# Input sums of the feed-forward's block products moved into the norming of token tiles and through DRAM, with the last down weights in other buffers

## The chip, the cores and the metric

One core of one Trainium2 chip runs the whole program. The metric is the device time of one execution in microseconds (us). The kernel before takes 3409.91 us, the median of three runs (3407.55 to 3410.49).

## What is computed

The reference is one step of a two-layer trunk on 256 context tokens and 1024 latent tokens of width 1024. Layer 0 mixes with a gated MLP and grouped-query attention, layer 1 with neighbourhood attention; after each mixer comes a SwiGLU feed-forward. Every sub-layer is normed before and after, and shifted, scaled and gated by six vectors that come from a conditioning vector (`mod_w`, `mod_b`). All arrays are float32. What the change touches is the output of a mixer and the feed-forward behind it:

```python
def sublayer_in(x, g, shift, scale):
    return rms_norm(x, g) * (1 + scale) + shift

def sublayer_out(x, y, g, gate):
    return x + gate * rms_norm(y, g)

def swiglu(h, w_in, w_out):
    g, u = jnp.split(h @ w_in, 2, axis=-1)
    return (jax.nn.silu(g) * u) @ w_out
```

with `w_in` of 1024 x 5632 and `w_out` of 2816 x 1024.

## The kernel before, in words

**Numbers.** A float32 operand is kept as two float32r parts, `hi` (a cast, on ACT) and `lo` (the rest, a subtraction on DVE or POOL); `split` (lines 168 to 176) makes both. A product is three matmuls: hi·hi, hi·lo, lo·hi. The normed, modulated activations of all 1280 tokens lie in `hh` and `hl`, eight blocks of 128 features by ten tiles of 128 tokens. Tiles 0 and 1 are the context, 2 to 9 the latents.

**Output projection and norms.** `out_proj` (line 1107) takes the token tiles in the order 4, 5, 6, 7, 8, 9, 2, 3, 0, 1 through a software pipeline: `load` (the attention output from DRAM and its split; layer 1 has it in `hh`/`hl` already), `product` (PE), `norms` (ACT's sums of squares, POOL's power at line 214, DVE's lines 414, 415 and 358) and `cols`. `cols` calls `prenorm_pair`: eight PE transposes (line 385), eight ACT passes (line 388) and the split into `hh`/`hl`; for an odd tile the features 0 to 511 first have the even tile of the pair subtracted (line 394). `cols` of tiles 0 and 1 is not done there but inside the feed-forward, as `before[0]` and `before[1]`. The subtraction of a split goes to POOL in layer 0 and to DVE in layer 1. Here the framework orders each engine's instructions itself, by program order and by when it thinks that they are ready.

**Feed-forward, up.** `ffn` (line 1168) makes gate and up projection of 128 + 128 columns of the 22 blocks `m` by seven block products (Strassen's scheme in Winograd's form) in place of eight: inputs are two halves of features by even and odd tiles, weights two halves of features by gate and up. Products 1, 5, 2 and 3 (`FREE`) read `hh`/`hl` as they are. Products 6, 7 and 4 (`BOUND`) need sums of input blocks, which `sums` (line 1174) forms once for each feed-forward: eight calls (four feature blocks by two token sets, set 0 = tiles 4 to 9, 384 columns for each product, set 1 = tiles 0 to 3, 256 columns). A call is seven DVE instructions (lines 1183 to 1191 and two split subtractions), three POOL (1187, 1188, 176) and three ACT casts. `weights` splits the weight block for a product, `weight_sums` (1206) forms the weight sums. PSUM has three banks of tag B, two double banks of tag A and one bank C. For the first two `m` all `FREE` products of set 0, then of set 1, then all `BOUND` ones run; from `m` = 2 on it is product by product. All of it stands in one hand-written list of (position, function) pairs, which are sorted by position (`at`, lines 1290 to 1341) and issued in that order on each engine (`weave`). `behind(("SP","DVE","PE"))` keeps the list's instructions on these three queues behind the last ones of `out_proj`; ACT and POOL have no such edge.

**Fillers.** `extra` runs steps of `mod_half_steps` (line 300): the next modulation vectors, by DVE multiply-adds (lines 320, 322), two small PE matmuls (327) and copies. In the main loop it is called once at even products and for two steps at odd ones. Layer 0's feed-forward carries six vectors (12 halves), layer 1's one.

**Feed-forward, down.** `gu_d` holds the 22 result blocks in DRAM. `down_load` (line 1348) loads and splits the weights and results of a pair of blocks. Pairs 0 to 7 are added up pair by pair over ten token tiles, and the last three pairs (`LAST = 3`) in one group, so that each tile is done and normed as it comes. The weights of a pair lie in the eight `wt` buffers, those of the last pair in `s5`, and the loads of pairs 9 and 10 come behind the loop and behind both `gate_load`s. Buffers: `wt` 8 x 4096 bytes for each partition, `raw` 3 x 4096, `s5` 17 x 5120, `t2` 5 x 2048.

**DMA.** All transfers are issued on SP's queue, in order: one that waits holds up those behind it.

Of the kernel before, what the change touches and what calls it, by code (L numbers as in the profile page):

```python
# [11 lines left out]
F32 = mybir.dt.float32  # L12
# [6 lines left out]
P = 128  # L19
# [30 lines left out]
def trunk_kernel(ctx: ExitStack, tc: tile.TileContext, A: dict, O: dict):  # L50
# [257 lines left out]
    def mod_half_steps(l, part):  # L308

        w, what = part // 3, part % 3  # L310
        for j in range(2):
            total = [t2([P, 512]) for _ in range(2)]
            for k in range(0, KT, 2):
                r = s5([P, 2, 512])
                SP.dma_start(r, A["mod_w"][l, k * P : k * P + 256, part * D + 512 * j : part * D + 512 * j + 512].rearrange("(b p) n -> p b n", b=2))
                yield
                for b in range(2):
                    for c in range(2):
                        if k + b == 0:
                            DVE.tensor_scalar(total[c], r[:, b], cond[:, k + b, c : c + 1], None, op0=ALU.mult)  # L320
                        else:
                            DVE.scalar_tensor_tensor(total[c], r[:, b], cond[:, k + b, c : c + 1], total[c], op0=ALU.mult, op1=ALU.add)  # L322
                    yield
            res, acc = t2([32, 512]), bank2()
            SP.dma_start(res, A["mod_b"][l, part, 32 * j : 32 * j + 32])
            for c in range(2):
                PE.matmul(acc[0:32, 0:512], pick[:, c, :], total[c], start=c == 0, stop=c == 1)
            yield
            DVE.tensor_tensor(res, acc[0:32, 0:512], res, op=ALU.add)
            yield  # L330
            if what == 2:
# [12 lines left out]
            yield  # L344
# [33 lines left out]
    def prenorm_pair(t, xh, l, w, lo):  # L378

        trs = []  # L380
        for _ in range(2):
            tr = bank((P, 4, P))
            trs += [tr[:, k, :] for k in range(4)]
# [5 lines left out]
        if t % 2 == 0:  # L389
            split(hh[:, :, rows(t)], hl[:, :, rows(t)], xh, lo, DVE)  # L390
        else:
            split(hh[:, 4:8, rows(t)], hl[:, 4:8, rows(t)], xh[:, 4:8], lo, DVE)
            for x in (hh, hl):
                DVE.tensor_tensor(xh[:, 0:4], xh[:, 0:4], f32(x[:, 0:4, rows(t - 1)]), op=ALU.subtract)
            split(hh[:, 0:4, rows(t)], hl[:, 0:4, rows(t)], xh[:, 0:4], lo, DVE)
# [712 lines left out]
    def out_proj(l, w, xsrc, dst, early=None):  # L1108

        w0, w1 = w[:4], w[4:]  # L1110
        gate = {}

# [32 lines left out]
        def cols(t):  # L1145
            prenorm_pair(t, st.pop(("xh", t)), l, 1, DVE if early else POOL)

        late = OUT_ORDER[-2:]
# [19 lines left out]
    def ffn(l, ubase, xsrc, dst, extra, before, after=()):  # L1168


        more, size = [], [(c.stop - c.start) * P for c in SETS]
        place = [slice(c.start * P, c.stop * P) for c in SETS]

        def sums(s, k):

            if not more:
                more.extend([[s5([P, 2, 640], F32R) for _ in range(2)] for _ in range(2)] for _ in range(3))
            q, n, c = SETS[s], size[s], place[s]
            tmp = s5([P, 3, n])
            x, d, z = (tmp[:, i].rearrange("p (q f) -> p q f", f=P) for i in range(3))  # L1180
            parts = [[more[i][a][k // 2][:, k % 2, c].rearrange("p (q f) -> p q f", f=P) for a in range(2)] for i in range(3)]
            b22, t1, b11, b21 = ([f32(v[:, r, q, e]) for v in (hh5, hl5)] for r, e in ((4 + k, 1), (k, 1), (k, 0), (4 + k, 0)))
            DVE.tensor_tensor(x, b22[0], t1[0], op=ALU.subtract)
            DVE.tensor_tensor(d, b22[1], t1[1], op=ALU.subtract)
            DVE.tensor_tensor(x, x, d, op=ALU.add)
            split(*parts[0], x, DVE)
            POOL.tensor_tensor(z, b21[0], x, op=ALU.subtract)
            POOL.tensor_tensor(z, z, b21[1], op=ALU.add)
            split(*parts[2], z, POOL)
            for v in b11:  # L1190
                DVE.tensor_tensor(d if v is b11[0] else d, x if v is b11[0] else d, v, op=ALU.subtract)  # L1191
            split(*parts[1], d, DVE)

        def tokens(i, s):

            if i in BOUND:
                parts = more[(6, 7, 4).index(i)]
                return [tuple(parts[a][k // 2][:, k % 2, place[s]] for a in range(2)) for k in range(4)]
# [8 lines left out]
        def weight_sums(m):  # L1207
# [4 lines left out]
            DVE.tensor_tensor(s1, u[:, 0], u[:, 1], op=ALU.add)  # L1212
            DVE.tensor_tensor(s3, g[:, 0], u[:, 0], op=ALU.subtract)
            if m == 0:
                ACT.copy(a22, u[:, 1])
            DVE.tensor_tensor(s2, s1, g[:, 0], op=ALU.subtract)  # L1216
            st["s", m] = {5: s1, 7: s3, 6: s2, 4: a22}

        def weights(m, i, lo=None):

            g = st["gu", m, 0]
            if i == 3:
                DVE.tensor_tensor(g[:, 1], g[:, 1], st["s", m][6], op=ALU.subtract)
            src = {1: g[:, 0], 2: g[:, 1], 3: g[:, 1]}[i] if i < 4 else st["s", m][i]
            st["w", m, i] = o = wt([P, 2, 512], F32R)
            split(o[:, 0], o[:, 1], src, lo or POOL)
# [64 lines left out]
        at(0.0, weights, 0, 1, DVE)  # L1291
        at(0.01, weight_sums, 0)
        for j, i in enumerate((5, 2, 3)):
            at(0.04 + 0.05 * j, weights, 0, i, POOL if j == 0 else DVE)
        at(0.2, before[0])
# [6 lines left out]
        at(0.95, weights, 1, 1)  # L1302
        at(1.6, weight_sums, 1)
        for j, i in enumerate((5, 2, 3)):
            at(1.7 + 0.25 * j, weights, 1, i)
# [3 lines left out]
        for k in range(4):  # L1309
            at(1.0 + 1.3 * k, sums, 0, k)  # L1310
            at(6.4 + 0.9 * k, sums, 1, k)
# [18 lines left out]
        for m in range(2, MT):  # L1330
            for j, i in enumerate(PRODUCTS):
# [4 lines left out]
                at(p + j + 0.45, extra, 2 if j % 2 else 1)  # L1336
# [11 lines left out]
        def down_load(j, make=None):  # L1348

            for m in (2 * j, 2 * j + 1):  # L1350
                r = raw([P, 1024])
                SP.dma_start(r, A["wall"][ubase + 3 * m + 2])
                w = [(make or wt)([P, 1024], F32R) for _ in range(2)]
# [40 lines left out]
        for j in range(n_pairs - LAST):  # L1394
            nxt = down_load(j + 1)
            for t in ORDER:
                for half in range(2):
                    finish(down((2 * j, 2 * j + 1), t, half))
                if t in (3, 7):
                    next(nxt, None)  # L1400
                extra(1)
            finish(nxt)
        extra(1000)
        for r in range(2):
            gate[r == 0] = gate_load(l, 1, r)
        for j in range(n_pairs - LAST + 1, n_pairs):
            finish(down_load(j, s5 if j == n_pairs - 1 else wt))
# [56 lines left out]
        for t in ORDER:  # L1464
            for half in range(2):
# [523 lines left out]
```

## Time and profile before

| | |
|---|---|
| median of the runs | 3409.91 us |
| the profiled execution's own time | 3409.43 us, span 3407.7 us |
| PE busy | 3172.5 us (93%) |
| DVE, POOL, ACT busy | 59%, 51%, 41% |
| DMA | 27.4% of 16 engines' span, 305 MB |
| granted TensorE clock, mean | 0.97 |

Times in the views are counted from the start of the span. The first feed-forward's up part lies at 701 to 1340 us, its down part up to 1660; the second's at 2474 to 3060 and up to the end. A group `L176 POOL TENSOR_TENSOR hl<-s,hh` is an instruction of line 176 on POOL that reads tiles `s` and `hh` and writes `hl`; square brackets give the idle time before it and what ended that. The granted clock is 1.00 at 2.4 GHz and 0.50 at 1.2 GHz.

### The profile page before, as it was taken

To read this page: it belongs to the slowest core of one execution; us is meant where nothing else is said; L and a number is where in the kernel's file an instruction comes from. 1 tells how busy PE (TensorE), PEld (TensorE's weight loads), DVE (VectorE), ACT (ScalarE), POOL (GpSimd) and SP (SyncE) were. 2 spreads that over 40 slices of the span, in tenths; PEclk is the share of its full clock that TensorE was granted. 3 is DMA by queue.
4 is the path that set the end of the run, shared out by engine and by line. 5 is a ranking of instruction groups with operands and counts; after the bars stand their busy time and mean duration, and the time that the engine had idled before them with its cause. 6 is when DMAs were issued, how large, how long until landed. Compare 5 with 4: busy or idle time off the path is not lost. (4 is left out here: it accounts for less than half of the span.)

```text
span 3407.7 us, 48787 instructions
## 1 busy us (share of the span) xinstructions
PE 3172.5 (93%) x18370; PEld 2783.4 (82%) x18370; DVE 1995.8 (59%) x3556; ACT 1410.8 (41%) x2959; POOL 1753.5 (51%) x1345
## 2 busy tenths in 40 slices
PE   7899998968999999998899999998959999999988
PEld 4678877858998999886678888887759999998867
DVE  4689987566676754443656666666676322224434
ACT  4488842533222223112456666666542333332111
POOL 4567764556565657434343333335156655565340
PEclk9999999979999999998999999999979999999989
DMA  6200134412333333323211111123313221224233
GB/s 225 76 23 20 44 110 150 140 59 98 106 112 118 126 116 120 104 84 111 102 51 46 47 48 47 47 64 120 112 50 113 68 77 65 75 77 130 85 104 114
DMA packets 145512, 305.41 MB, mean 90 GB/s; under 512 B 12654, under 2 KB 70894, under 8 KB 145276
## 3 DMA queue, kind: packets, MB, share of 16 engines
q1 hardware_dynamic: 145276, 302.29, 27.4%
q8 instruction: 144, 2.36, 0.3%
q14 instruction: 92, 0.75, 0.1%
HBM read 237.59 MB, written 64.65 MB: 89 GB/s over the span
## 5 line engine op out<-in xcount | busy, mean ns | idle before, releaser
L176 POOL TENSOR_TENSOR w<-raw,w 128x512 fp32r<-128x512 f32 (+1 forms) x299 | 461.6, 1554 | 361.3 <-ACT w L175 356.4
L1166 PE MATMUL B<-hh,w 128*128 128x384 f32 (+1 forms) x2112 | 530.8, 326 | 38.4 <-ACT s L1262 12.8
L1166 PE MATMUL A<-s,w 128*128 128x384 f32 (+1 forms) x3168 | 492.3, 311 | 14.4 <-DVE s L1254 14.1
L1166 PEld LDWEIGHTS A<-s,w 128*128 128x128 f32 x3168 | 476.4, 189 | 20.3 <-DVE s L1254 15.4
L1166 PEld LDWEIGHTS B<-hh,w 128*128 128x128 f32 x2112 | 381.6, 194 | 49.7 <-ACT s L1262 13.4
L175 ACT CAST w<-raw 128x512 fp32r<-128x512 f32 (+1 forms) x308 | 203.5, 689 | 457.4 <-DVE raw L1216 278.6
L1166 PE MATMUL B<-hl,w 128*128 128x384 f32 (+1 forms) x1056 | 342.0, 324 | 0.0
L190 PE MATMUL B<-w,hh 128*128 128x512 f32 x576 | 231.8, 402 | 24.6 <-ACT w L175 17.8
L322 DVE SCALAR_TENSOR_TENSOR t<-s,c,t 128x512 f32<-128x512 f32 x196 | 221.0, 1177 | 46.8 <-DMA s<-mod_w 46.8
L1386 DVE TENSOR_TENSOR s<-s,B 128x512 f32<-128x512 f32 x192 | 132.1, 688 | 186.3 <-PE B L192 186.3
L214 POOL TENSOR_TENSOR sm<-sm,c 128x1 f32<-128x1 f32 (+2 forms) x110 | 86.4, 786 | 297.4 <-DVE sm L213 296.0
L191 PE MATMUL B<-w,hh 128*128 128x512 f32 x576 | 230.1, 399 | 6.2 <-POOL w L176 6.2
L460 PE MATMUL B<-c,s 128*128 128x128 f32 x1344 | 207.7, 278 | 27.7 <-DVE raw L442 14.3
L192 PE MATMUL B<-w,hl 128*128 128x512 f32 x576 | 229.3, 398 | 0.0
L176 POOL TENSOR_TENSOR hl<-raw,hh 128x640 fp32r<-128x640 f32 (+1 forms) x84 | 128.0, 1526 | 195.0 <-ACT hh L175 187.5
L190 PE MATMUL C<-hh,w 128*128 128x512 f32 (+1 forms) x576 | 212.5, 369 | 3.3 <-ACT s L135 1.2
L460 PEld LDWEIGHTS B<-c,s 128*128 128x128 f32 x1344 | 156.2, 141 | 68.6 <-DVE raw L442 17.5
L476 DVE TENSOR_TENSOR t<-B,t 128x512 fp32r<-128x512 f32 (+2 forms) x216 | 127.5, 590 | 143.2 <-ACT t L470 129.6
L192 PE MATMUL C<-hh,w 128*128 128x512 f32 (+1 forms) x576 | 205.2, 356 | 2.8 <-POOL w L176 2.8
L1166 PEld LDWEIGHTS B<-hl,w 128*128 128x128 f32 x1056 | 204.8, 194 | 0.0
L191 PE MATMUL C<-hl,w 128*128 128x512 f32 (+1 forms) x576 | 204.5, 355 | 0.0
L832 POOL TENSOR_TENSOR s<-s,sm 128x640 f32<-128x640 f32 x128 | 156.8, 1256 | 62.8 <-DVE sm L830 45.8
(356 smaller groups left out, 7864.4 us busy)
## 6 DMA issues: line engine op xcount, KB each, us to landing
raw<-wall SPq DMA_DIRECT2D x147, 512.0 KB, 3.5
s<-mod_w SPq DMA_DIRECT2D x56, 512.0 KB, 5.5
raw<-gu_d SPq DMA_DIRECT2D x88, 320.0 KB, 2.8
gu_d<-s SPq DMA_DIRECT2D x44, 384.0 KB, 3.2
raw<-x_d SPq DMA_DIRECT2D x30, 512.0 KB, 3.6
raw<-mod_w SPq DMA_DIRECT2D x24, 512.0 KB, 3.7
gu_d<-s SPq DMA_DIRECT2D x44, 256.0 KB, 3.2
w<-wall SPq DMA_DIRECT2D x22, 512.0 KB, 4.3
```

What stands on the lines that cost most here:

```text
L175: ACT.copy(hi, src)
L176: (eng or DVE).tensor_tensor(lo, src, f32(hi), op=ALU.subtract)
L190: PE.matmul(out, sh, mh, start=i == 0, stop=False)
L191: PE.matmul(out, sh, ml, start=False, stop=False)
L192: marks["PE"] = PE.matmul(out, sl, mh, start=False, stop=i == n - 1)
L214: POOL.tensor_tensor(r, v, mhalf[:, 0:n], op=ALU.pow)
L322: DVE.scalar_tensor_tensor(total[c], r[:, b], cond[:, k + b, c : c + 1], total[c], op0=ALU.mult, op1=ALU.add)
L460: PE.transpose(tr[:, at : at + P], self.p[a][:, col : col + P], ident)
L476: DVE.tensor_tensor(tl[:, 0:n], tr[:, 0:n], f32(th[:, 0:n]), op=ALU.subtract)
L832: POOL.tensor_tensor(p[:, c], p[:, c], z.to_broadcast([P, 640]), op=ALU.mult)
L1166: PE.matmul(out, x, z, start=start and i + j == 0, stop=i == n - 1 and j == 2, skip_group_check=True)
L1386: DVE.tensor_tensor(yt, yt, part, op=ALU.add)
```

## The change

The sums of inputs are no longer formed in the feed-forward. When `prenorm_pair` handles an odd tile, it forms the three sums of the pair for all four feature blocks: four POOL instructions of 128 x 512, one of them before the split of the odd tile, the others behind it. Three DMAs store them into a new DRAM tensor `t_d`. The feed-forward loads them (twelve DMAs: three sums by two halves by two token sets) and splits each (twelve ACT casts, eight DVE and four POOL subtractions). The buffer for two of the sums is an `s5` in layer 0 and a `wt` in layer 1 (`s5` for tiles 0 and 1). The transposes of tiles 0 and 1 go to a double bank A in place of two banks B.

The weight sums and splits of block 0 all go to POOL, and their order in the list changes; `before[0]` comes right behind them. The third weight of block 1 that was split behind its sums is split before them.

A filler half has one more empty step between its last multiply-add and its PE matmuls, and the two steps at odd products become two calls half a product apart.

In the down part, the weights of blocks 18, 19 and 20 lie in `s5`, block 21's in `wt`, and pairs 8, 9 and 10 are all loaded during pair 7. The latents' gate is loaded behind that loop, the context's gate at tile 8 of the last group.

```diff
 mod_half_steps:
                         else:
                             DVE.scalar_tensor_tensor(total[c], r[:, b], ...)
                     yield
+            yield
             res, acc = t2([32, 512]), bank2()
...
+    t_d = [dr.tile([3, P, 4, 640], F32, name=f"t_d{l}") for l in range(2)]
+
+    def prenorm_pair(t, xh, l, w, lo, make, wide):
+        if wide:
+            tr = bank2((P, KT, P))
+            trs = [tr[:, k, :] for k in range(KT)]
+        else:
...
         if t % 2 == 0:
             split(hh[:, :, rows(t)], hl[:, :, rows(t)], xh, lo, DVE)
-        else:
-            split(hh[:, 4:8, rows(t)], hl[:, 4:8, rows(t)], xh[:, 4:8], lo, DVE)
-            for x in (hh, hl):
-                DVE.tensor_tensor(xh[:, 0:4], xh[:, 0:4], f32(x[:, 0:4, rows(t - 1)]), op=ALU.subtract)
-            split(hh[:, 0:4, rows(t)], hl[:, 0:4, rows(t)], xh[:, 0:4], lo, DVE)
+            return
+        a, b = xh[:, 0:4], xh[:, 4:8]
+        more = make([P, 2, 4, P])
+        POOL.tensor_tensor(more[:, 0], b, a, op=ALU.subtract)
+        split(hh[:, 4:8, rows(t)], hl[:, 4:8, rows(t)], b, lo, DVE)
+        for x in (hh, hl):
+            DVE.tensor_tensor(a, a, f32(x[:, 0:4, rows(t - 1)]), op=ALU.subtract)
+        split(hh[:, 0:4, rows(t)], hl[:, 0:4, rows(t)], a, lo, DVE)
+        POOL.tensor_tensor(b, b, a, op=ALU.subtract)
+        POOL.tensor_tensor(more[:, 1], f32(hh[:, 4:8, rows(t - 1)]), b, op=ALU.subtract)
+        POOL.tensor_tensor(more[:, 1], more[:, 1], f32(hl[:, 4:8, rows(t - 1)]), op=ALU.add)
+        for i, src in enumerate((b, more[:, 0], more[:, 1])):
+            SP.dma_start(t_d[l][i][:, :, rows(t // 2)], src)
...
         def cols(t):
-            prenorm_pair(t, st.pop(("xh", t)), l, 1, DVE if early else POOL)
+            prenorm_pair(t, st.pop(("xh", t)), l, 1, DVE if early else POOL, wt if early and t not in late else s5, t in late)
...
 ffn:
-        def sums(s, k):
...
+        def sums_load(i, h, s):
+            st["t", i, h, s] = r = (t2 if s else s5)([P, 2, size[s]])
+            SP.dma_start(r, t_d[l][i][:, 2 * h : 2 * h + 2, place[s]])
+
+        def sums_split(i, h, s):
+            if s == 0:
+                more[i][h] = [s5([P, 2, 640], F32R) for _ in range(2)]
+            hi, lo = (x[:, :, place[s]] for x in more[i][h])
+            split(hi, lo, st.pop(("t", i, h, s)), POOL if i == 1 else DVE)
...
 weight_sums, weights:
+            eng = DVE if m else POOL
+            eng.tensor_tensor(s1, u[:, 0], u[:, 1], op=ALU.add)
             if m == 0:
+                weights(m, 5)
+                weights(m, 2)
                 ACT.copy(a22, u[:, 1])
+            else:
+                DVE.tensor_tensor(s3, g[:, 0], u[:, 0], op=ALU.subtract)
+            eng.tensor_tensor(s2, s1, g[:, 0], op=ALU.subtract)
+            if m == 0:
+                weights(m, 3)
+                POOL.tensor_tensor(s3, g[:, 0], u[:, 0], op=ALU.subtract)
...
-        at(0.0, weights, 0, 1, DVE)
-        at(0.01, weight_sums, 0)
-        for j, i in enumerate((5, 2, 3)):
-            at(0.04 + 0.05 * j, weights, 0, i, POOL if j == 0 else DVE)
-        at(0.2, before[0])
+        at(0.0, weights, 0, 1)
+        at(0.02, weight_sums, 0)
+        at(0.04, before[0])
...
+        at(1.0, weights, 1, 2)
         at(1.6, weight_sums, 1)
-        for j, i in enumerate((5, 2, 3)):
+        for j, i in enumerate((5, 3)):
             at(1.7 + 0.25 * j, weights, 1, i)
...
-        for k in range(4):
-            at(1.0 + 1.3 * k, sums, 0, k)
-            at(6.4 + 0.9 * k, sums, 1, k)
+        for j, (i, h) in enumerate((i, h) for i in range(3) for h in range(2)):
+            at(0.5 + 0.7 * j, sums_load, i, h, 0)
+            at(2.6 + 0.7 * j, sums_split, i, h, 0)
+            at(6.3 + 0.7 * j, sums_load, i, h, 1)
+            at(7.5 + 0.7 * j, sums_split, i, h, 1)
...
-                at(p + j + 0.45, extra, 2 if j % 2 else 1)
+                at(p + j + 0.45, extra, 1)
+                if j % 2:
+                    at(p + j + 0.95, extra, 1)
...
 down_load:
-                w = [(make or wt)([P, 1024], F32R) for _ in range(2)]
+                w = [(s5 if MT - 5 < m < MT - 1 else wt)([P, 1024], F32R) for _ in range(2)]
...
         for j in range(n_pairs - LAST):
-            nxt = down_load(j + 1)
+            nxt = itertools.chain(*(down_load(i) for i in ([j + 1] if j < n_pairs - LAST - 1 else range(j + 1, n_pairs))))
...
-                if t in (3, 7):
+                if t in (3, 7) or j == n_pairs - LAST - 1:
                     next(nxt, None)
                 extra(1)
+            if j == n_pairs - LAST - 2:
+                extra(1000)
             finish(nxt)
-        extra(1000)
-        for r in range(2):
-            gate[r == 0] = gate_load(l, 1, r)
-        for j in range(n_pairs - LAST + 1, n_pairs):
-            finish(down_load(j, s5 if j == n_pairs - 1 else wt))
+        gate[False] = gate_load(l, 1, 1)
...
         for t in ORDER:
+            if t == 8:
+                gate[True] = gate_load(l, 1, 0)
```

## Rows read from the trace of the kernel before

**Rows 1.** Stretches: busy us of PE, PEld, DVE, ACT, POOL; granted clock, DMA share, GB/s.

```profile
700.70:800.20 99.50, 59.46 (x288) 55.63 (x287) 70.86 (x86) 35.74 (x79) 60.02 (x53) 0.76 0.12 37
2473.60:2573.00 99.40, 61.18 (x298) 57.29 (x299) 72.64 (x93) 35.02 (x79) 54.36 (x51) 0.76 0.13 43
2650.00:2700.00 50.00, 50.00 (x345) 50.00 (x344) 13.96 (x26) 15.03 (x30) 28.96 (x27) 1.00 0.22 69
830.00:1330.00 500.00, 488.30 (x3191) 461.01 (x3190) 313.43 (x431) 137.04 (x279) 307.23 (x243) 0.99 0.34 114
1500.00:1550.00 50.00, 50.00 (x216) 40.09 (x215) 24.80 (x36) 7.63 (x9) 21.93 (x12) 1.00 0.30 87
...
3300.00:3328.00 28.00, 16.22 (x50) 11.61 (x50) 2.77 (x5) 7.85 (x10) 16.01 (x9) 0.70 0.41 123
600.00:700.00 100.00, 98.57 (x459) 80.31 (x458) 56.99 (x60) 49.15 (x104) 51.74 (x37) 1.00 0.44 141
2395.00:2473.00 78.00, 68.92 (x329) 56.28 (x328) 56.32 (x83) 44.92 (x102) 13.24 (x19) 0.99 0.39 124
```

**Rows 2.** What PE waited for, 700.7 to 800.3 us: total us, times, longest.

```profile
PE B L385 <- ACT s L388: 7.4, 1, 7.4
PE B L1166 <- ACT s L1262: 6.6, 1, 6.6
PE B L1166 <- DVE w L176: 4.2, 1, 4.2
```

**Rows 3.** Groups on DVE and POOL, 700.7 to 800.2 us: busy us, mean ns.

```profile
L176 DVE TENSOR_TENSOR s<-s,s 128x384 fp32r<-128x384 f32 (+1 forms) x16 | 12.2, 761 | 8.6 <-ACT s L175 8.6
...
L176 POOL TENSOR_TENSOR w<-raw,w 128x512 fp32r<-128x512 f32 x8 | 11.3, 1414 | 5.6 <-ACT w L175 5.6
```

**Rows 4.** Start of the first feed-forward in order of time, DVE and ACT.

```profile
705.78 0.68 DVE L176 TENSOR_TENSOR w<-raw,w 128x512 fp32r<-128x512 f32 x1
...
711.89 0.62 ACT L175 CAST w<-raw 128x512 fp32r<-128x512 f32 x1 [3.14 <-DVE raw L1223]
```

**Rows 5.** First down part, last group, in order of time: ACT, PE, POOL, DVE.

```profile
1577.16 1.04 ACT L175 CAST w<-raw 128x1024 fp32r<-128x1024 f32 x1
...
1578.25 0.80 PE L190 MATMUL B<-w,hh 128*128 128x512 f32 x1 [8.09 <-ACT w L175]
...
1578.83 2.34 POOL L176 TENSOR_TENSOR w<-raw,w 128x1024 fp32r<-128x1024 f32 x1
...
1593.18 0.69 DVE L1386 TENSOR_TENSOR s<-s,B 128x512 f32<-128x512 f32 x1 [23.70 <-PE B L192]
...
1599.10 0.68 DVE L1386 TENSOR_TENSOR s<-s,B 128x512 f32<-128x512 f32 x1
```

**Rows 6.** What PE waited for, 830 to 1330 us: total us, times, longest.

```profile
PE A L327 <- DVE t L322: 11.4, 10, 4.2
```

**Rows 7.** First output projection, an odd tile's step in order of time: POOL, DVE.

```profile
620.92 1.69 POOL L176 TENSOR_TENSOR hl<-s,hh 128x512 fp32r<-128x512 f32 x1 [3.47 <-DVE hh L173]
622.97 1.30 POOL L176 TENSOR_TENSOR hl<-s,hh 128x512 fp32r<-128x512 f32 x1 [0.36 <-DVE sm L213]
624.24 0.55 POOL L214 TENSOR_TENSOR sm<-sm,c 128x1 f32<-128x1 f32 x1
624.75 2.40 POOL L176 TENSOR_TENSOR s<-raw,s 128x1024 fp32r<-128x1024 f32 x1
...
624.82 2.88 DVE L358 TENSOR_SCALAR s<-s,sm 128x1024 f32<-128x1024 f32 x1 [1.86 <-POOL sm L214]
```

**Rows 8.** Second output projection in order of time: POOL, DVE.

```profile
2440.96 2.37 POOL L402 TENSOR_TENSOR w<-w,raw 128x1024 f32<-128x1024 f32 x1
...
2442.35 2.07 DVE L415 TENSOR_TENSOR s<-s,raw 128x1024 f32<-128x1024 f32 x1
```

**Rows 9.** DMA issues of the page: count, KB each, median us to landing.

```profile
raw<-wall SPq DMA_DIRECT2D x147, 512.0 KB, 3.5
...
gu_d<-s SPq DMA_DIRECT2D x44, 256.0 KB, 3.2
```

More of the change, by code (lines that the diff above doesn't have):

```diff
@@ L376, in prenorm_cols @@
         split(hh[:, :, rows(t)], hl[:, :, rows(t)], xh, lo or POOL, DVE)
[L378 to L383, printed above, removed]
+    t_d = [dr.tile([3, P, 4, 640], F32, name=f"t_d{l}") for l in range(2)]
[4 more added lines that the diff above has]
+        else:
+            trs = []
+            for _ in range(2):
+                tr = bank((P, 4, P))
+                trs += [tr[:, k, :] for k in range(4)]
         for k in range(KT):
@@ L1111, in out_proj @@
         gate = {}
+        late = OUT_ORDER[-2:]
         def load(t):
@@ L1145, in cols @@
         def cols(t):
-            prenorm_pair(t, st.pop(("xh", t)), l, 1, DVE if early else POOL)
-        late = OUT_ORDER[-2:]
+            prenorm_pair(t, st.pop(("xh", t)), l, 1, DVE if early else POOL, wt if early and t not in late else s5, t in late)
         pipeline(OUT_ORDER, (0, load), (1, product), (3 if early else 2, lambda t: t in late or cols(t)), (1, norms))
@@ L1168, in ffn @@
     def ffn(l, ubase, xsrc, dst, extra, before, after=()):
-        more, size = [], [(c.stop - c.start) * P for c in SETS]
+        more, size = [[None, None] for _ in range(3)], [(c.stop - c.start) * P for c in SETS]
         place = [slice(c.start * P, c.stop * P) for c in SETS]
-        def sums(s, k):
[L1176 to L1192, printed above, removed]
+        def sums_load(i, h, s):
[6 more added lines that the diff above has]
+            split(hi, lo, st.pop(("t", i, h, s)), POOL if i == 1 else DVE)
         def tokens(i, s):
@@ L1197, in tokens @@
                 parts = more[(6, 7, 4).index(i)]
-                return [tuple(parts[a][k // 2][:, k % 2, place[s]] for a in range(2)) for k in range(4)]
+                return [tuple(parts[k // 2][a][:, k % 2, place[s]] for a in range(2)) for k in range(4)]
             k0, e = {1: (0, 0), 5: (0, 1), 2: (4, 0), 3: (4, 1)}[i]
@@ L1211, in weight_sums, with weights @@
             s3, s2, a22 = (t2([P, 512]), t2([P, 512]), t2([P, 512])) if m == 0 else (u[:, 0], g[:, 0], u[:, 1])
-            DVE.tensor_tensor(s1, u[:, 0], u[:, 1], op=ALU.add)
-            DVE.tensor_tensor(s3, g[:, 0], u[:, 0], op=ALU.subtract)
+            eng = DVE if m else POOL
+            eng.tensor_tensor(s1, u[:, 0], u[:, 1], op=ALU.add)
+            st["s", m] = {5: s1, 7: s3, 6: s2, 4: a22}
             if m == 0:
+                weights(m, 5)
+                weights(m, 2)
                 ACT.copy(a22, u[:, 1])
-            DVE.tensor_tensor(s2, s1, g[:, 0], op=ALU.subtract)
-            st["s", m] = {5: s1, 7: s3, 6: s2, 4: a22}
-        def weights(m, i, lo=None):
+            else:
[4 more added lines that the diff above has]
+                POOL.tensor_tensor(s3, g[:, 0], u[:, 0], op=ALU.subtract)
+        def weights(m, i):
             g = st["gu", m, 0]
             if i == 3:
-                DVE.tensor_tensor(g[:, 1], g[:, 1], st["s", m][6], op=ALU.subtract)
+                (DVE if m else POOL).tensor_tensor(g[:, 1], g[:, 1], st["s", m][6], op=ALU.subtract)
             src = {1: g[:, 0], 2: g[:, 1], 3: g[:, 1]}[i] if i < 4 else st["s", m][i]
             st["w", m, i] = o = wt([P, 2, 512], F32R)
-            split(o[:, 0], o[:, 1], src, lo or POOL)
+            split(o[:, 0], o[:, 1], src, POOL)
         banks = {}
@@ L1346, in ffn, with down_load @@
         gate, started = {}, set()
-        def down_load(j, make=None):
+        def down_load(j):
             for m in (2 * j, 2 * j + 1):
```

## The prediction

> **What bounds the kernel now.** I read the busy time by stretch first. PE is busy all the time and at 2.4 GHz in the main loop of the second feed-forward (345 matmuls in 50 us, 0.145 us each) and in the down part (216 in 50 us, 0.2315 us each) [rows 1]. So a microsecond counts only where PE stands still. Three kinds of places do, and the change touches all of them. At the start of each feed-forward 99.5 us hold 59 to 61 us of PE work at a mean clock of 0.76 [rows 1]. At the last group of each down part 28 us hold 16 us at 0.70 [rows 1]. In the first main loop PE lacks 11.7 us of 500 [rows 1].
>
> The list of PE's waits then says on what. In the start it waits for ACT's passes on the late tiles (banks B), for the SiLU of block 0 (bank B again) and for the first weight [rows 2]. The order of time shows that these are queue effects: the first weight's `lo` runs on DVE only at 705.78, behind the last tile's norms, and ACT, which must do the late tiles, stands 3.14 us before a weight cast that waits for DVE [rows 4]. DVE is busy 70.9 of the 99.5 us, and POOL 60 [rows 1].
>
> **The change, part by part.** The sum is made against the profiled execution's own 3409.43 us, 0.48 us below the median of the runs.
>
> *Start of the feed-forward.* Its floor: 14 products by two sets by 12 matmuls are 336; at 0.145 us [rows 1] that is 48.7 us, and 16 transposes add about 2. So at most 99.5 - 50.7 = 48.8 us are to be had in each. DVE loses eight calls of seven instructions; two of the seven are the 16 subtractions of 12.2 us [rows 3]. It gets eight subtractions of 128x768 or 128x512, some 7 us. POOL loses 24 instructions and gets four, but it also takes block 0's weights and the late pair's sums, and its list becomes the longest. I walk it with 1.41 us for a 128x512 subtraction [rows 3]. POOL comes to it at 701.8, when tile 3's sums are done (the step of [rows 7] 74 us later, with 3 us of sums more). Eight instructions for block 0 (first weight, s1, two splits, s2, its use, third split, s3) end at 713; a full split of tile 0 takes 2.6 (twice 1.3 [rows 7]) and two splits of block 1 2.8; tile 1's six instructions 8.4; an addition for product 5, 1.0; then comes block 1's second weight, ready at 729.3. PE has done five of the 28 products by then and waits. The other 23 are 276 matmuls, 40 us, so the stretch ends at 769.3, or 771 with matmuls at half clock behind the waits. That is 29 us less; the second start has two or three POOL splits fewer and DVE ones more, and I take 29 again: **-58**. Transposes into banks A cost nothing, since both are empty until product 6. The twelve loads (3.5 us to landing for a larger one [rows 9]) lie beside products; four or more of set 0 stand on SP behind the late pair's three stores, which wait for POOL until about 727, and still land by 733, before the first bound product at about 746. If POOL were 15 us later, they would be late next. Bounds for one start: 48 (the floor) and 12 (POOL's list grows longer by DVE's holding it up).
>
> *Last group of the down part.* DVE has fetched the last result of pair 7 at 1569.5 (1593.18 less 23.70 idle) and the third of the new group only from 1599.1 on [rows 5]. Three half tiles are 54 matmuls, 12.5 us at 0.2315; 17.1 us are over, of which I leave 1.7 to DVE's own queue (an estimate): 15.4 us are lost. The reason is buffers: blocks 18 and 19 have been loaded but wait for `wt` until pair 7 is done; the cast comes at 1577.16, PE starts at 1578.25, POOL's `lo` at 1578.83 [rows 5]. With `s5` three blocks can be split during pair 7. POOL then has three weights and six results there (3 x 2.34 [rows 5], and 6 x 1.46, the same for 640 of 1024 columns: 15.8 us) beside pair 8's 4.7, in 28 us; eleven loads through three `raw` buffers at about 7 us a turn (3.5 landing [rows 9], cast, subtraction, queue) take 26. Only block 21 waits for pair 7: cast 1.04 and `lo` 2.34 [rows 5] against 3.5 us of PE work on the other five blocks. I leave 1.4 and gain 14 in each; the second's stretch is the same [rows 1]: **-28**. Bounds 9 and 15.4. The gate loads, moved behind, are needed 8 us later and are covered by the first tile.
>
> *Fillers.* The empty step puts a whole product between the last multiply-add and the matmuls, so the 11.4 us of ten waits [rows 6] go, and with them some matmuls at half clock (mean 0.99 over 500 us [rows 1], at most 5 us): **-13**, bounds 8 and 16. The steps rise from 184 to 196, and the loop has 200 calls, so none spills over.
>
> *First output projection.* Here the change adds: four POOL instructions and three stores in each pair, four pairs outside the late one. PE is full (98.6 of 100 us), POOL half [rows 1]. In an odd step POOL idles 3.47 us before the first split, where the first sum fits; then two splits with 0.36 us between them, the power for the next norm, and the next tile's split until 627.15 [rows 7]. Three sums of 1.3 us (the duration of the same shape there [rows 7]) go ahead of the power, since they come earlier in the program: 3.9 - 0.36, 3.5 us later. DVE's row 358 ends 0.55 us behind POOL's last split, at 627.70 [rows 7], when PE is due for its transposes. So there is no slack and the 3.5 us pass to PE, with half a microsecond at half clock: **+16** for four pairs. Bounds 0 (POOL's gaps take the sums) and 36 (9 for a pair, if the next tile's load waits as well).
>
> *Second output projection.* DVE is busy 56 of 78 us, POOL 13, PE 69 [rows 1]: DVE is close to being the bound. A POOL instruction holds it up: line 415, issued at 2442.35, ends 1.09 us after POOL's end at 2443.33 [rows 8]. Four sums are 5.2 us of POOL in each pair. Some lie beside DVE's work on PSUM; I take 3 of the 5.2, over four pairs: **+12**. Bounds 0 and 21. The Trainium skill, page "SBUF — State Buffer", section "SBUF: two separate sides", says that a DVE instruction with two SBUF inputs and a GpSimd instruction that reads SBUF exclude each other for the whole instruction; the row agrees, and by that rule alone all 5.2 us of each pair would pass, 20.8 in place of 12.
>
> Stores of `t_d` (3.2 us to landing for as many bytes [rows 9]) are behind no reader there.
>
> **Sum:** 3409.4 - 58 - 28 - 13 + 16 + 12 = **3338 us**.
>
> **Rivals.** A difference under 0.2% (7 us) is no change here.
> (a) POOL takes DVE's place. In the start it has almost no gap, DVE's splits stand behind its instructions, SP's loads behind the late stores. Each start then gains 12: 3338 + 34 = 3372 us. For it: POOL already 60 of 99.5 us busy [rows 1]. Against: DVE's 56 instructions are gone, 12.2 us in 16 of them [rows 3].
> (b) The sums vanish in POOL's gaps: it is half idle in the first output projection and more in the second [rows 1]. Then the 28 us of cost go: 3310 us. Against it stands the missing slack behind 627.15 [rows 7].
> (c) Slower: the stores hold up SP. In an odd step of an output projection the next tile's load stands behind three stores that wait for POOL, and its buffer behind them. Then a pair costs the sums 3.9, a store 3.2, a load 3.5, cast 1.04 and split 2.4, 14.1 us; eight pairs 113, against 99 won: 3423 us. It decides above 12.4 us a pair. Against it: loads come a tile ahead, and the stores need not be issued first.
> (d) The trip through DRAM gives the starts nothing, since the bound products now wait for stores and loads: 3338 + 58 = 3396 us.
>
> **How the numbers follow.** Chances: the forecast 0.55, (a) 0.20, (b) 0.14, (c) 0.05, (d) 0.06. The forecast alone spans 3320 to 3358. The range runs from 3292, below (b) with a start nearer its floor, to 3380, above (a); outside it lie (c), (d) and some of the tails. Faster 0.92, same 0.03, slower 0.05.
>
> **What would show it.** Right: starts of some 70 us, with POOL busiest and PE waiting for a weight on POOL; DVE idle between the last two groups for under 8 us; line 327 gone from PE's waits; 3 to 4 us of new waits on line 358 or on the split at odd tiles of the first output projection. Wrong: starts still of 85 us or more, PE waiting there on loads of `t_d`, or new waits of over 10 us for a pair.

## The result, and the profile after

The changed kernel takes 3361.8 us (median of 4 runs, 3359.3 to 3365.4), the kernel before, run beside it, 3410.2 us (3407.6 to 3415.7): a ratio of 0.9857, 95% interval 0.984 to 0.9874. That is 48 us less; the prediction had 71. The time lies inside its range, but outside the span of the forecast alone (3320 to 3358). The profiled spans are 3407.7 and 3358.9 us.

The first table sets the stretches side by side, each in us between two instructions that both kernels have: the first and the last squares of a product in an output projection (row 352 before, 353 after), the last fetch of block 1 in a start (row 1276, 1291), the first result of a down part, the first key subtraction of the attention behind it, the end. Here and below a stretch is that of one profiled execution.

| stretch | before | after | change | predicted |
|---|---|---|---|---|
| first output projection | 108.8 | 126.3 | +17.6 | +16 |
| first start | 107.1 | 82.9 | -24.2 | -29 |
| first main loop | 538.0 | 522.3 | -15.7 | -13 |
| first down part | 365.0 | 359.0 | -6.0 | -14 |
| second output projection | 77.9 | 87.5 | +9.6 | +12 |
| second start | 107.2 | 84.8 | -22.4 | -29 |
| second main loop | 496.6 | 496.1 | -0.5 | 0 |
| second down part | 331.4 | 323.7 | -7.7 | -14 |

The rest of the two spans differs by 0.6 us. Stretches of the changed kernel in the view by windows (busy us of PE, PEld, DVE, ACT, POOL; granted clock, DMA share, GB/s):

```profile
600.00:700.00 100.00, 88.06 (x383) 70.70 (x382) 44.15 (x49) 41.38 (x88) 58.00 (x42) 0.93 0.45 138
...
719.00:802.00 83.00, 60.24 (x354) 58.23 (x353) 36.37 (x38) 37.23 (x74) 68.72 (x53) 0.86 0.38 124
...
850.00:1350.00 500.00, 499.22 (x3241) 473.23 (x3240) 314.44 (x435) 141.78 (x283) 320.78 (x249) 1.00 0.36 120
```

Against [rows 1]: in the start DVE fell from 71 to 36 us and POOL became the busiest engine. The main loop is full, 499.2 of 500 us at a clock of 1.00, where 488.3 stood. The first output projection, once full at 1.00, lacks 12 us of 100 and lost 0.07 of its clock. What PE waits for in the whole kernel (total us, times, longest):

```profile
PE B L1183 <- ACT s L1277: 17.3, 2, 9.3
...
PE B L191 <- POOL w L176: 13.7, 2, 7.2
PE B L394 <- DVE sm L213: 11.2, 3, 3.8
...
PE A L190 <- DVE s L431: 8.0, 5, 2.8
```

These four lie in the four places that fell short of the forecast or lost time: the starts (a SiLU on ACT), the last groups of the down parts (a weight on POOL), the first and the second output projection. No wait of PE names a load of `t_d`.

### The profile page after: what moved, and what is told of

The parts are those of the page before. It is cut to its first block, busy times and chain, and to the rows that moved or that the text cites. A ratio compares the mean times of both kernels' runs of the same rounds, so it can differ in the third digit from the quotient of the medians.

```text
span 3358.9 us, 48818 instructions
## 1 busy us (share of the span) xinstructions
PE 3166.4 (94%) x18370; PEld 2785.2 (83%) x18370; DVE 1933.6 (58%) x3446; ACT 1404.4 (42%) x2935; POOL 1801.9 (54%) x1359
## 5 line engine op out<-in xcount | busy, mean ns | idle before, releaser
L1183 PE MATMUL B<-hh,w 128*128 128x384 f32 (+1 forms) x2112 | 523.2, 323 | 35.0 <-ACT s L1277 17.3
L191 PE MATMUL B<-w,hh 128*128 128x512 f32 x552 | 220.2, 399 | 13.7 <-POOL w L176 13.7
L190 PE MATMUL B<-w,hh 128*128 128x512 f32 x552 | 221.2, 401 | 8.4 <-DVE s L1404 8.4
L192 PE MATMUL B<-w,hl 128*128 128x512 f32 x552 | 219.8, 398 | 0.0
```

Source lines behind the costliest of these rows:

```text
L190: PE.matmul(out, sh, mh, start=i == 0, stop=False)
L191: PE.matmul(out, sh, ml, start=False, stop=False)
L192: marks["PE"] = PE.matmul(out, sl, mh, start=False, stop=i == n - 1)
L1183: PE.matmul(out, x, z, start=start and i + j == 0, stop=i == n - 1 and j == 2, skip_group_check=True)
```

## The experiments

Medians in us, ratios to the kernel before with 95% intervals, and the stretches of the first table that the runs speak of (P1, P2 the projections, S1, S2 the starts, D1, D2 the down parts). Two profiles can differ by 1 to 2 us in a stretch that no edit touches (P1 is 126.3 in e5 and 124.7 in e7), so smaller differences say nothing.

| run | median | ratio | P1 | S1 | D1 | P2 | S2 | D2 |
|---|---|---|---|---|---|---|---|---|
| e1_fillers | 3395.4 | 0.9957 [0.9942, 0.9972] | 108.8 | 107.0 | 368.3 | 77.9 | 106.8 | 332.0 |
| e2_down | 3393.4 | 0.9953 [0.9937, 0.9969] | 108.7 | 107.0 | 358.2 | 77.9 | 107.1 | 323.4 |
| e3_no_sums | 3328.8 | 0.9765 [0.9751, 0.978] | 108.7 | 80.1 | 358.1 | 77.5 | 83.0 | 324.4 |
| e4_gate_dve | 3362.1 | 0.9858 [0.9841, 0.9874] | 126.4 | 82.8 | 359.6 | 87.5 | 84.4 | 324.8 |
| e7_gate_behind | 3347.1 | 0.9814 [0.9799, 0.9828] | 124.7 | 84.1 | 353.8 | 87.5 | 87.0 | 316.1 |
| e5_tile1_late | 3363.3 | 0.9864 [0.9849, 0.9878] | 126.3 | 85.2 | 359.0 | 87.6 | 84.8 | 324.8 |
| e6_sums_behind | 3370.7 | 0.9879 [0.9863, 0.9896] | 122.7 | 85.0 | 358.2 | 92.0 | 92.3 | 324.8 |
| e8_all | 3360.2 | 0.9852 [0.9838, 0.9867] | 122.6 | 85.4 | 353.3 | 90.2 | 89.1 | 320.2 |
| e9_five_behind | 3341.7 | 0.9796 [0.978, 0.9813] | 112.2 | 86.4 | 354.4 | 87.5 | 86.9 | 317.6 |
| e10_late_dve | 3349.3 | 0.9816 [0.9801, 0.983] | 124.7 | 84.4 | 354.3 | 87.5 | 86.3 | 316.5 |
| e11_dve | 3343.4 | 0.9803 [0.9778, 0.9828] | 122.1 | 79.7 | 352.3 | 87.5 | 83.9 | 316.5 |
| e12_best | 3334.8 | 0.978 [0.9763, 0.9796] | 112.1 | 81.9 | 352.8 | 87.5 | 85.1 | 319.4 |

**Two parts of the change alone.** On the kernel before, e1 has the lines of the fillers, e2 those of the down part, as the diff above shows them.

> The kernel before with the fillers' part alone (the empty step in the conditioning filler and the two single calls in place of a double one). In the changed kernel the first main loop became 15.7 us shorter. Theory: that is the fillers' part by itself, so 3410 - 15 = 3395 us (3392 to 3398), and the ten waits on the multiply-add (11.4 us) are under 2 us. As the prediction put it, -13, 3397 us. Rival: a part of the 15.7 comes from the new start of the feed-forward (the first iterations of the loop find their weights earlier); then this kernel gains 8 us or less.

> The kernel before with the down part's part alone (blocks 18 to 20 in other buffers, the last six blocks' loads in one chain, the gate loads moved behind). The prediction's term is -28: 3382 us, with DVE idle under 8 us between the last two groups. Theory after the changed kernel's trace: the gate multiply stands on GpSimd ahead of the last block's subtraction, so PE waits 6.5 to 7.2 us once in each down part, and the part is worth -6 and -8 us, 3396 us (3392 to 3400). Rival: the part is worth its 28 us by itself and loses them in the changed kernel to something else there; then 3382 us and no wait of over 3 us.

e1 gains 15 us; its main loop shrinks from 538.0 to 521.6. The fillers' term is theirs alone. (Its first down part, which has none of the edits, is 3.3 us longer, at a clock of 0.95 in place of 0.97; why is not known.) e2 gains 17, not 28 (its down parts lose 6.8 and 8.0), with one wait of 7.3 and one of 6.6 us on POOL's subtraction: the theory.

The start's edits (sums gone from DVE, block 0's weights on POOL, tiles 0 and 1 through banks A, one weight earlier) were not run apart. Which of them brings the 24 and 22 us is read from rows, not shown.

**Down part: the gate ahead of the last weight.** In order of time in the changed kernel (start, us; the idle time before it and what ended it in brackets):

```profile
1553.21 2.34 POOL L419 TENSOR_TENSOR s<-s,raw 128x1024 f32<-128x1024 f32 x1 [2.31 <-DMA raw<-gpost]
1555.51 2.34 POOL L176 TENSOR_TENSOR w<-raw,w 128x1024 fp32r<-128x1024 f32 x1
...
1559.16 0.69 DVE L1404 TENSOR_TENSOR s<-s,B 128x512 f32<-128x512 f32 x1 [11.41 <-PE B L192]
1565.40 0.69 DVE L1404 TENSOR_TENSOR s<-s,A 128x512 f32<-128x512 f32 x1 [5.55 <-PE A L192]
```

DVE's idle time ahead of the group's results is 11.4 us against 23.7 in [rows 5]. What is left begins on POOL: the gate's multiply waits 2.31 us for its load, takes 2.34, and block 21's `lo` stands behind it, though its cast had ended at 1549.8.

```diff
 e4: -        POOL.tensor_tensor(g, g, gp, op=ALU.mult)
     +        (eng or POOL).tensor_tensor(g, g, gp, op=ALU.mult)   # eng=DVE for gate[False]
 e7: +        with behind(after):                                 # after block 21's lo
              POOL.tensor_tensor(g, g, gp, op=ALU.mult)
```

> The changed kernel with one instruction on another engine: the latents' gate in each down part is multiplied on VectorE in place of GpSimd. Theory: the last block's subtraction then starts when its cast is done (1.0 us later than 1548.75 by the changed kernel's clock) in place of 1555.5, PE's single waits of 7.2 and 6.5 us fall to about 2.5, and with the half clock behind them each down part is 5 us shorter: 3362 - 10 = 3352 us. Rival A: the wait is set by the last block's transfer or cast, so nothing changes (3360 to 3364). Rival B: VectorE now stands for the gate's load and holds a bank, so PE waits there in place of it: 3358 us or more.

> The changed kernel with the latents' gate still multiplied on GpSimd, but behind the last block's subtraction in each down part, nothing else moved. Put on VectorE it had stood there 12.5 us for its load and held PE 8.2 us, which told nothing of the theory. Theory: the subtraction ends at 1553.3 in place of 1557.85, PE's single waits of 7.2 and 6.5 us fall to 2.5 and 2, with the half clock behind them 5 us in each: 3352 us (3349 to 3355). Rival A: the wait is set by the last block's transfer or cast: 3360 to 3364. Rival B: the gate is now late for the first tile's VectorE multiply, and the tail gives the gain back: 3358 us or more.

e4 brought nothing. The multiply then stood on DVE ahead of results of pair 7, waited 12.53 us for its load, and PE waited 8.2 us for a bank: its rival B, with the same cause on another queue. e7 left the multiply on POOL, behind the subtraction:

```profile
1550.55 2.34 POOL L176 TENSOR_TENSOR w<-raw,w 128x1024 fp32r<-128x1024 f32 x1
1553.41 2.38 POOL L422 TENSOR_TENSOR s<-s,raw 128x1024 f32<-128x1024 f32 x1 [0.52 <-DMA raw<-gpost]
...
1554.21 0.69 DVE L1407 TENSOR_TENSOR s<-s,B 128x512 f32<-128x512 f32 x1 [6.61 <-PE B L194]
```

PE's waits fall from 7.2 and 6.5 us to 2.4 and 1.5, and the kernel gains 14.7 us against the changed one (11.2 by the spans). From the kernel before to e7 the down parts lose 365.0 - 353.8 and 331.4 - 316.1, together 26.5 us.

**Output projections: what the sums cost and by what.** An odd step of the first projection in the changed kernel, POOL, then DVE:

```profile
654.73 1.48 POOL L408 TENSOR_TENSOR s<-s 128x512 f32<-128x512 f32 x1 [2.42 <-issue]
656.17 1.30 POOL L176 TENSOR_TENSOR hl<-s,hh 128x512 fp32r<-128x512 f32 x1
657.43 1.26 POOL L409 TENSOR_TENSOR s<-hh,s 128x512 f32<-128x512 f32 x1
658.65 0.55 POOL L214 TENSOR_TENSOR sm<-sm,c 128x1 f32<-128x1 f32 x1
659.17 1.26 POOL L410 TENSOR_TENSOR s<-s,hl 128x512 f32<-128x512 f32 x1
660.38 2.81 POOL L176 TENSOR_TENSOR s<-raw,s 128x1024 fp32r<-128x1024 f32 x1
663.16 0.54 POOL L214 TENSOR_TENSOR sm<-sm,c 128x1 f32<-128x1 f32 x1
...
659.23 1.74 DVE L359 TENSOR_SCALAR s<-s,sm 128x1024 f32<-128x1024 f32 x1 [3.71 <-POOL sm L214]
...
663.73 1.28 DVE L431 SCALAR_TENSOR_TENSOR s<-A,sm,s 128x1024 f32<-128x1024 f32 x1 [2.70 <-POOL sm L214]
```

As forecast, sums stand ahead of the power (658.65), and row 359 follows the power; of the three, two are there and the third (row 410) comes behind it. The second power, at 663.16, is late as well, behind that sum and a whole split of the next heads. The stretch as a whole, before and after, in the view by windows:

```profile
592.40:701.20 108.80, 107.37 (x499) 87.51 (x498) 60.55 (x65) 52.54 (x110) 53.47 (x39) 1.00 0.43 136
```

```profile
593.00:719.30 126.30, 113.88 (x496) 91.32 (x494) 58.30 (x64) 52.70 (x109) 71.62 (x53) 0.95 0.42 134
```

PE waits three times there for some 3.7 us (11.2 in the list above), once for each of the first three pairs. It is also busy 6.5 us longer for the same matmuls, at a clock of 0.95 in place of 1.00. The fourth pair's sums, those of tile 3, end at 722.8, in the first start.

```diff
 e3: sums only `if wide`; stores of (b, a, b) otherwise
 e6: rows 408 to 410 and the stores in a function, called a step later behind the last power
 e9: also    -  POOL.tensor_tensor(more[:, 0], b, a, op=ALU.subtract)
             +  POOL.tensor_tensor(more[:, 0], b, f32(hh[:, 0:4, rows(t - 1)]), op=ALU.subtract)
             +  POOL.tensor_tensor(more[:, 0], more[:, 0], f32(hl[:, 0:4, rows(t - 1)]), op=ALU.subtract)
     b's sum behind the even tile's first power, four behind the next heads' split; layer 0, with e7
```

> The changed kernel without the four GpSimd sums of the four pairs that are not late, in each output projection; the three stores of each pair stay and write other data, so the bound products of those tokens are computed from wrong sums. Theory: the sums alone cost what the two output projections lost, 16.2 and 9.6 us: 3362 - 26 = 3336 us (3330 to 3342); the first projection, from its first product to its last squares, falls from 138 to 122 us. Rival A: the stores and their buffers cost it (SP stands for GpSimd, the next load comes late); with the sums gone and the stores kept the gain is under 8 us, 3354 us or more. Rival B: the loss is the half clock behind the waits, in the first projection alone; then 3346 us.

> The changed kernel with three of the four GpSimd sums of the four pairs that are not late, and the stores, issued behind the second power of the next tile, where GpSimd stood idle for 4.15 us in the first output projection; the first sum stays where it is. Theory: the sums cost by their place in GpSimd's queue, ahead of the powers; the first projection, 126.3 us from first to last squares in the changed kernel and 108.7 without sums, falls to 112, the second, 87.5 against 77.5, to 85: 3362 - 17 = 3345 us (3340 to 3350). Rival A: the sums hold VectorE up by running beside it, wherever they stand; then both projections stay within 4 us of what they were, 3358 us or more. Rival B: now they hold up the split of the next tile's output heads, behind which PE waits; no gain or a loss in the first projection alone.

> The changed kernel with the gate behind (3347 us), and in the first output projection alone nothing of the sums left ahead of an odd tile's splits: the first sum is formed later from the others in two instructions, so five in place of four, one of them before the even tile's split and four behind the next output heads' split; the late pair and the second projection as in the changed kernel. Moving three of four had brought only 3.7 us of 17.6 there. Theory: what counts is the place ahead of a power or of a split; with none of that left, the first projection falls from 125 to 112 us, 3347 - 13 = 3334 us (3330 to 3340). Rival A: a GpSimd sum lengthens the VectorE instruction that runs beside it (a cast of 0.43 took 1.5 us, row 359 2.8 in place of 1.75), wherever it stands: the projection stays above 119 us, 3341 us or more. Rival B: GpSimd has no room for five: the powers come late, nothing gained or a loss.

Without the sums both projections are back at their old length, 108.7 and 77.5, although the stores stay: the sums cost 17.6 and 10.0 us. The starts get 2.8 and 1.8 shorter too, since tile 3's sums stood there on POOL, and the kernel is 33 us faster, more than the 26 expected.

e6 was a miss: its first projection gave back 3.7 us, and the second lost 4.5, the start behind it 7.5. The first sum still stood ahead of the splits, and the next heads' split, now behind the sums, made PE wait 4.2 us. In e9 no sum is ahead of an odd tile's splits or of the power behind them, and the projection takes 112.2 us against e7's 124.7, though POOL does a sum more. So the place in the queue sets most of the cost, not POOL's load. The gain over e7 is 5.4 us (8.9 by the spans) and not 13, so the time misses the theory's range and lies at rival A's bound, while the projection is the theory's. Tile 3's five sums now lie at the head of the first start, where PE waits 6.3 us for its second weight and which is 2.3 us longer; the two down parts are 2.1 us longer together, which is not explained.

In the second projection the other mechanism is seen, in the changed kernel (POOL, then DVE), and in e3 a like step without sums:

```profile
2412.80 1.64 POOL L403 TENSOR_TENSOR w<-s 128x512 f32<-128x512 f32 x1 [0.31 <-ACT s L397]
...
2417.15 1.27 POOL L408 TENSOR_TENSOR s<-s 128x512 f32<-128x512 f32 x1
...
2413.20 1.52 DVE L173 CAST hh<-s 128x512 fp32r<-128x512 f32 x1
...
2417.22 1.28 DVE L431 SCALAR_TENSOR_TENSOR s<-A,sm,w 128x1024 f32<-128x1024 f32 x1 [0.44 <-POOL sm L214]
...
2418.75 2.33 DVE L432 TENSOR_TENSOR s<-s,raw 128x1024 f32<-128x1024 f32 x1
2421.00 1.79 DVE L176 TENSOR_TENSOR hl<-s,hh 128x512 fp32r<-128x512 f32 x1
```

```profile
2390.44 0.42 DVE L173 CAST hh<-s 128x512 fp32r<-128x512 f32 x1
2390.89 0.69 DVE L176 TENSOR_TENSOR hl<-s,hh 128x512 fp32r<-128x512 f32 x1
...
2393.69 1.22 DVE L434 TENSOR_TENSOR s<-s,raw 128x1024 f32<-128x1024 f32 x1
```

The cast, the addition and the split's subtraction (row 176) are 1.1 us longer each beside POOL's sums, 3.3 us in this pair. Row 431, which reads a PSUM bank, takes the same 1.28 us beside a sum as in e3. Three of the four pairs lie in the stretch here too.

**Starts: queue or load?** In order of time in the changed kernel, ACT, DVE, POOL, PE:

```profile
748.50 0.62 ACT L175 CAST w<-t 128x512 fp32r<-128x512 f32 x1 [6.16 <-DVE t L1221]
753.52 0.62 ACT L175 CAST w<-raw 128x512 fp32r<-128x512 f32 x1 [4.41 <-DVE raw L1238]
754.16 1.28 ACT L1277 ACT_TABLE_LOAD   x1
755.45 0.58 ACT L1277 ACTIVATE s<-B,c 128x384 f32<-128x384 f32 x1
...
744.89 1.78 DVE L406 TENSOR_TENSOR s<-s,hh 128x512 f32<-128x512 f32 x1 [2.41 <-POOL s L403]
...
743.59 1.27 POOL L403 TENSOR_TENSOR s<-s 128x512 f32<-128x512 f32 x1
...
755.52 1.27 POOL L176 TENSOR_TENSOR w<-t,w 128x512 fp32r<-128x512 f32 x1
...
756.09 0.69 PE L1183 MATMUL B<-hh,w 128*128 128x384 f32 x1 [8.01 <-ACT s L1277]
```

PE, with five of the 28 products done, waits 8 us for a bank that the SiLU of block 0 must empty. ACT had stood twice for DVE's sums of block 1's weights, DVE for POOL's first sum of tile 1, which no product of set 0 needs. But POOL's subtraction for the weight of the same product ends only at 756.79, 0.7 us behind PE's start: without the wait for the SiLU, PE would have waited for POOL.

```diff
 e5:  -        at(1.45, before[1])
      +        at(2.0, before[1])
 e10: the late pair's four sums on DVE; with e7          e11: and all of layer 0's
 e12: e9, tile 3's and the late pair's sums on DVE, at(2.25, before[1])
```

> The changed kernel with tile 1's column step put at 2.0 in place of 1.45 in the feed-forward's order, so behind block 1's weight sums, casts and subtractions. Theory: in the changed kernel ACT stands 6.2 and 4.4 us for VectorE's sums of block 1's weights, VectorE stands for GpSimd's first sum of tile 1, and so the SiLU of block 0 and PE (8.0 us in the first start, 9.3 in the second) wait for tile 1, which no product of set 0 needs. With the step later these waits fall to about 2, each start is 6 us shorter: 3362 - 12 = 3350 us (3346 to 3354). Rival A, the prediction's bound: GpSimd's list as a whole is the limit, so PE's wait only moves to block 1's second weight: 3358 us or more. Rival B: the late pair's stores now hold SP's loads back and the bound products wait for them: slower than 3362 us.

> The changed kernel with the gate behind (3347 us) and the late pair's four sums, those in the starts, on VectorE in place of GpSimd. Moving tile 1 back left the starts as long as they were, 85 us with GpSimd busy for 88% of it. Theory, now that of the prediction: GpSimd's list is the bound of the starts. Four instructions of 1.3 to 1.7 us fewer on it and four of 0.7 more on VectorE (busy 46%) make each start 4 to 6 us shorter: 3337 us (3333 to 3341). Rival A: the chain of queues (ACT for VectorE, VectorE for GpSimd) sets it and not GpSimd's sum of work: under 2 us in each, 3343 us or more. Rival B: VectorE with sums in its queue brings block 1's weights later still: slower than 3347 us.

> As the kernel with the late pair's sums on VectorE, and the first output projection's sums on VectorE too; the second projection's stay on GpSimd. Theory: GpSimd is the queue on which the norms' powers and the splits wait, VectorE has gaps of 2 to 6 us in each step; four sums of 0.7 us there cost at most 1.5 us a pair, so the first projection falls from 125 to 113 us and the time to 3337 - 12 = 3325 us (3320 to 3332). Rival: the sums delay row 359 on VectorE by as much as they did the power on GpSimd (2.8 us a pair and half clock behind it): the projection stays above 119 us, 3331 us or more.

> The changed kernel with the gate behind, five sums behind in the first three pairs of the first output projection, the sums of tile 3 and of the late pair on VectorE in both layers, and tile 1's column step at 2.25, behind the SiLU of block 0 on ACT. Theory: two limits lie close together in the starts, the chain of queues that ends at the SiLU and GpSimd's list; taking away the first alone (tile 1 later) or part of the second alone (the late sums on VectorE) gave nothing, and both together shorten the starts from 84 and 87 us to 78 and 82. With the first projection at 113 this gives 3330 us (3326 to 3335). Rival A: the starts are bound by something else still, the norms of the last tile and the first weight, so they stay at 80 and 84 as without tile 3's sums: 3337 us. Rival B: VectorE is now the late queue: 3342 us or more.

e5 moved the wait and gained nothing. PE's waits in its start:

```profile
PE B L1183 <- ACT s L1266: 8.8, 2, 7.1
PE A L1183 <- DVE s L1269: 5.8, 1, 5.8
...
PE B L1183 <- ACT s L1277: 4.0, 1, 4.0
```

The SiLU's wait fell from 8.0 to 4.0, and POOL's weight was ready 5.9 us ahead of PE's start there; but the copy of row 1266 grew from 6.2 to 8.8 and row 1269 from 3.0 to 5.8. e10 took four instructions off POOL and gained nothing either. e11 brought the first start to 79.7, as e3 did, but the projection stays at 122.1, its rival: PE still waits 10.4 us there at the transposes, for DVE. (Its four times scatter from 3336 to 3354; the stretches are those of the shortest.) In e12 POOL has 62.4 us in 82, 6 fewer than in the changed kernel, and the start takes 81.9; its time lies in the theory's range, but its starts (81.9 and 85.1) are nearer to rival A's 80 and 84 than to 78 and 82:

```profile
704.00:786.00 82.00, 61.42 (x356) 59.09 (x357) 43.45 (x47) 36.79 (x74) 62.40 (x47) 0.85 0.39 125
```

Its main wait is now for the copies of row 1266 (1292 there), 11.1 us in three. The longest in order of time, ACT, then PE:

```profile
717.29 0.62 ACT L175 CAST w<-raw 128x512 fp32r<-128x512 f32 x1 [4.61 <-POOL raw L1264]
...
721.59 0.53 ACT L1292 COPY s<-B 128x384 f32<-128x384 f32 x1
...
722.17 0.69 PE L1209 MATMUL B<-hh,w 128*128 128x384 f32 x1 [5.54 <-ACT s L1292]
```

So neither POOL's load nor one chain is the limit: whenever one wait is taken away, the next copy or SiLU is late on ACT, whose queue has it behind weight casts that stand for DVE or POOL. That ACT's order is the bound is argued from these rows, not shown; a kernel with the fetches ahead of the casts was not run, and the bound of the starts stays open.

The edits of e5, e6 and e7 in one kernel:

> The three edits together: tile 1 late, three sums and the stores behind, the gate behind. If the three theories hold and their gains add, 3362 - 12 - 17 - 10 = 3323 us. If only places that stay queues of GpSimd are concerned and it is short of time as a whole, the gains overlap in the starts: 3335 us or more.

It is 13 us slower than e7 alone: tile 1 gains nothing, and e6's losses in the second projection and the start behind it stay, in part; the second down part is 4.1 us longer too, which is not explained. e12 is the fastest of the kernels that form all sums, 3334.8 us, a ratio of 0.978 to the kernel before.

## Why the prediction was right, and where it fell short

*Sign and size.* Faster, inside the range, 24 us behind the forecast: 11 are missing in the starts and 14 in the last groups. The range reaches that far only for rival (a)'s 3372, whose cause bears on the starts alone; that it holds the time is in part luck. Of the signs named, line 327's waits are gone but for one of 0.7 us, and new waits of 3.7 us stand in the first projection; the starts take 83 and 85 us and not some 70, and DVE idles 11.4 us between the last groups and not under 8.

*Starts, -29 each, -24.2 and -22.4.* DVE was unburdened and POOL is the busiest engine, as forecast; the loads of `t_d` hide, so rival (d) fell. What failed is the walk of POOL's list, which gives POOL no wait for another engine. PE does stop after five of the 28 products, as forecast, but for the SiLU on ACT. Block 1's second weight, that of its product 5, ready 28.1 us behind the last squares in the walk (729.3 less 701.2), is ready 37.4 us behind them (756.79 less 719.34), after 7.2 us in which POOL stood idle for DVE and ACT. From that stop on the start takes 46.2 us (802.25 less 756.09), 42 in the walk and 66.6 in the kernel before (808.29 less 741.73):

```profile
741.73 0.69 PE L1166 MATMUL B<-hh,w 128*128 128x384 f32 x1 [6.63 <-ACT s L1262]
```

So 20 of the 24 us are won behind the fifth product. The walk ended after 70 us, the runs after 80 to 92: it was off by more than its term, which was counted from a stretch of 99.5 us that ends 8 us ahead of block 1's last fetch. The walk left out ACT, whose queue has tile passes, weight casts and the fetches of banks in one order, and DVE, on which block 1's sums stand behind tile 1's subtraction. It is rival (a) in part: DVE behind POOL's instructions, at 5 to 7 us a start instead of 17.

*Last groups, -14 each, -6.0 and -7.7.* The failed step is "the gate loads, moved behind, are needed 8 us later and are covered by the first tile". They are covered for their reader; but the multiply stands on POOL ahead of block 21's `lo`. With that one instruction behind, the two terms are 26.5 us, close to the forecast's 28.

*Fillers, -13.* 15.7 in the loop and 15 alone; the ten waits are gone but for one of 0.7 us. The slower clock behind them was worth 4.8 us (PE was busy for 526.3 us of the loop before and for 521.5 after, with the same matmuls), where 1.6 were taken.

*First projection, +16.* 17.6, with the mechanism as told: sums ahead of the power, no slack behind row 358, a lower clock after the waits. But the closeness is partly luck. The sum has four pairs at 4.0 us, and three lie in the stretch, at 5.9: the waits are of 3.7 us (3.5 forecast), and the slower clock costs 2.2 and not half a microsecond. The price was too low and the count too high; tile 3's pair, counted here, had been put into the start's walk as well. That the cost is one of place is shown by e9, which gives 12.5 of it back against e7 with more work.

*Second projection, +12.* 9.6; without the sums 77.5, so they are the cause. The price was right, 3.2 us a pair where 3 were taken, and the count was not: three pairs lie in the stretch. If, by the rule of the Trainium skill, page "SBUF — State Buffer", section "SBUF: two separate sides", all of POOL's 5.2 us in each pair had passed, three pairs would have cost 15.6. The lengthened rows agree with its exclusion, but the stretch lost 9.6: part of the sums lies beside work of DVE that they don't hold up, such as row 431.

*Rival (c).* No wait of PE in the projections names a load, and a pair lost 5.9 and 3.2 us (17.6 and 9.6 over three), not 14.1.

## What to carry to other kernels

When an instruction moves, walk every queue that it enters for what stands behind it there, and not only for its own reader: one gate multiply, whose reader came over 10 us later, cost half of a term. An engine that is half idle still charges for work put ahead of a short instruction on the critical chain (here a power of 0.55 us); put such work behind that chain, even at one instruction more. Where several engines hand work round in a circle, as in the starts here, the list of one engine bounds the time from below but does not give it. Where a price is taken times a count, check both: here a price too low and a count too high gave a sum that looked right.

## What the runs showed of the hardware that was not expected

DVE's cast from SBUF to SBUF, with one input, is held up by POOL as the additions with two inputs are: 1.52 us in place of 0.42, and it ends 0.28 us behind POOL's sum (2412.80 + 1.64). The same goes for the scaling of a tile by a scalar: in the first projection row 359 took 1.74 us, in e6 beside a POOL split 2.83, and 0.76 in the second. The Trainium skill, in the section named above, counts copies, casts and scalings in a mode with two ports among what excludes POOL; that these ran in such a mode no run shows, but their lengthening agrees with it. The forecast had used its words on two inputs alone.
